# Row softmax on one core: chunks grouped in pairs of 32 rows a partition, with one paired load and one paired store

## The chip, the cores and the metric

The kernel runs on one core of one Trainium2 chip. The metric is the device time of one execution in microseconds. The engines that matter are the vector engine (DVE), the scalar engine (ACT), the sync engine (SP), which here only issues DMAs, and the 16 DMA engines that move data between the device memory (HBM) and the on-chip memory (SBUF, 128 partitions). DMAs issued from SP go through one DMA queue (q1 in the profile), those issued from ACT through another (q10).

## The reference

The input is a float32 tensor of 16 x 1024 rows of 512 numbers, 33.55 MB; the output has the same shape. Each row gets a softmax at temperature 0.5:

```python
def reference(x):
    temp = 0.5
    x_scaled = x / temp
    x_max = np.max(x_scaled, axis=-1, keepdims=True)
    exp_x = np.exp(x_scaled - x_max)
    return (exp_x / np.sum(exp_x, axis=-1, keepdims=True)).astype(np.float32)
```

## The kernel before

The 16384 rows are cut into 8 chunks of 2048 rows. In a chunk, each of the 128 partitions holds G = 16 consecutive rows of 512 numbers, so one chunk is 4 MiB, and one partition's part of it is one contiguous piece of 32 KiB in HBM. This text counts chunks from 0, as the code does; the wording "chunks 5+6" of the change's author counts from 1 and means chunks 4 and 5 here, and "chunks 3+4" means 2 and 3.

The tables at the top of the kernel say how each chunk is moved and worked on. `LOADS` cuts chunk 0 into two loads, rows 0 to 4 and 4 to 16; every other chunk is one load. `BLOCKS` cuts chunk 0 into three blocks of work and chunk 7 into two; the rest are one block each, 11 blocks in all. `STORES` has one store a chunk. Six chunk buffers exist (`BUFS = 6`), and results overwrite the input in place; chunks 6 and 7 reuse the buffers of chunks 0 and 1, so their loads wait for the stores of these chunks.

For each block, four steps follow each other:

- `shift`: issues the chunk's loads from SP when the chunk is first met (L66), takes the negated maximum of each row on DVE (L74), and multiplies it by 2 on DVE (L78) to make the bias;
- `exponentials`: on ACT, one instruction for each of the block's rows a partition (L86) computes exp(2x + bias) in place and leaves the sum;
- `scale_vector` and `scale_scalar`: DVE takes the reciprocal of the sums (L101) and multiplies seven eighths of the rows (L103); ACT multiplies the rest (L112);
- `store`: ACT issues the chunk's store (L120) once its last block is done.

The order is written out by hand (`manual_schedule`), and each engine works through its instructions in program order. The maxima run two blocks ahead of the scaling, and the exponentials one block ahead:

```python
    for i in range(n):
        if i + 1 < n:
            exponentials(i + 1, rows(i + 1)[0])
        scale_vector(i)
        scale_scalar(i)
        if i + 2 < n:
            shift(i + 2)
        store(i)
```

Loads are issued as early as their buffers allow: SP has nothing else to do, so the loads of chunks 0 to 5 all go out in the first microseconds and stand in line in SP's queue.

Of the kernel before, what the change touches and what calls it, by code (L numbers as in the profile page):

```python
# [1 line left out]

# [4 lines left out]


@with_exitstack
def kernel(  # L10
    ctx: ExitStack,
    tc: tile.TileContext,
    x: bass.AP,
    out: bass.AP,
):
    nc = tc.nc
    fp32 = mybir.dt.float32
    P = nc.NUM_PARTITIONS
    AX = mybir.AxisListType.X
    EXP = mybir.ActivationFunctionType.Exp  # L20
    COPY = mybir.ActivationFunctionType.Copy
    MAX = mybir.AluOpType.max

    D = x.shape[-1]
    xf = x.flatten_outer_dims()
    of = out.flatten_outer_dims()
    N = xf.shape[0]

    G = 16
    C = N // (P * G)
    assert C * P * G == N
    xr = xf.rearrange("(c p g) d -> c p g d", p=P, g=G)
    outr = of.rearrange("(c p g) d -> c p g d", p=P, g=G)
    WHOLE = [(0, G)]
    LOADS = [[(0, 4), (4, G)]] + [WHOLE] * 7
    BLOCKS = [[(0, 4), (4, 8), (8, G)]] + [WHOLE] * 6 + [[(0, 8), (8, G)]]
    STORES = [WHOLE] * 8  # L40
    BMAX = 16
    BUFS = 6

    data = ctx.enter_context(tc.tile_pool(name="data", bufs=BUFS))
    stats = ctx.enter_context(tc.tile_pool(name="stats", bufs=6))

    ctx.enter_context(tc.manual_schedule())


    warm = stats.tile([P, 1], fp32, name="warm", bufs=1)  # L50
    nc.vector.memset(warm, 0.0)  # L51
    nc.scalar.activation(out=warm, in_=warm, func=EXP)  # L52

    chunks = {}
    blocks = [(c, lo, hi) for c in range(C) for lo, hi in BLOCKS[c]]
    n = len(blocks)
    biases, sums, recips = {}, {}, {}

    def load(c):
        if c < BUFS:  # L60
            chunks[c] = data.tile([P, G, D], fp32, name="xt")
        else:
            chunks[c] = chunks[c - BUFS]
        xt = chunks[c]
        for lo, hi in LOADS[c]:
            nc.sync.dma_start(out=xt[:, lo:hi, :], in_=xr[c][:, lo:hi, :])  # L66

    def shift(i):
        c, lo, hi = blocks[i]
        if c not in chunks:  # L70
            load(c)
        b = hi - lo
        negmax = stats.tile([P, BMAX], fp32, name="negmax")
        nc.vector.tensor_reduce(  # L74
            negmax[:, 0:b], chunks[c][:, lo:hi, :], axis=AX, op=MAX, negate=True
        )
        biases[i] = stats.tile([P, BMAX], fp32, name="bias")
        nc.vector.tensor_scalar_mul(biases[i][:, 0:b], negmax[:, 0:b], 2.0)  # L78

    def exponentials(i, rows):  # L80
        c, lo, hi = blocks[i]
        if i not in sums:
            sums[i] = stats.tile([P, BMAX], fp32, name="sums")
        for g in rows:
            row = chunks[c][:, lo + g, :]
            nc.scalar.activation(  # L86
                out=row,
                in_=row,
                func=EXP,
                bias=biases[i][:, g : g + 1],  # L90
                scale=2.0,
                accum_out=sums[i][:, g : g + 1],
            )


    def scale_vector(i):
        c, lo, hi = blocks[i]
        b = hi - lo
        k = b - b // 8
        recips[i] = stats.tile([P, BMAX], fp32, name="recip")  # L100
        nc.vector.reciprocal(recips[i][:, 0:b], sums[i][:, 0:b])  # L101
        rows = chunks[c][:, lo : lo + k, :]
        nc.vector.tensor_mul(  # L103
            rows, rows, recips[i][:, 0:k].unsqueeze(2).broadcast_to((P, k, D))
        )

    def scale_scalar(i):
        c, lo, hi = blocks[i]
        b = hi - lo
        for g in range(b - b // 8, b):  # L110
            row = chunks[c][:, lo + g, :]
            nc.scalar.activation(  # L112
                out=row, in_=row, func=COPY, scale=recips[i][:, g : g + 1]
            )

    def store(i):
        c, _, end = blocks[i]
        for lo, hi in STORES[c]:
            if hi == end:
                nc.scalar.dma_start(  # L120
                    out=outr[c][:, lo:hi, :], in_=chunks[c][:, lo:hi, :]
                )

    shift(0)
    shift(1)

    def rows(i):
        c, lo, hi = blocks[i]
        cut = hi - lo - (2 if c == 1 else 0)
        return range(cut), range(cut, hi - lo)  # L130

    exponentials(0, rows(0)[0])
# [9 lines that stand above are left out]
            exponentials(i + 1, rows(i + 1)[1])  # L142


# [1 line left out]
_INS = ['x']  # L146
_OUTS = [((16, 1024, 512), 'float32')]


# [23 lines left out]
```

## Time and profile before

| quantity | value |
|---|---|
| median of 4 runs | 162.27 us (162.16 to 162.35) |
| the profiled execution's own time | 162.16 us |
| its span in the profile | 160.4 us |
| DVE busy | 134.6 us (84%) |
| ACT busy | 102.2 us (64%) |
| bytes read from HBM, written to HBM | 33.55 MB, 33.55 MB |
| mean rate over the span | 419 GB/s |
| a reduce of 16 rows a partition (L74) | 8.68 us |
| a DVE scaling of 14 rows a partition (L103) | 7.62 us |
| an exponential of one row a partition (L86) | 0.71 us, and 0.19 us for its sum |

Times inside the profile are microseconds from the start of the span. The profiled execution took 1.76 us more than its span. The profile also names, for each DMA queue, the packets, the bytes and the share of the 16 DMA engines' time that its packets took, and the trace keeps start, duration and size of every packet. "Landing" is the moment at which a DMA has reported its completion.

### The profile page before, as it was taken

The page shows a single profiled execution, that of the slowest core. Times are in us where ns is not written, and L with a number is a line of the kernel's source. Part 1 is how long each engine was busy: PE and PEld are TensorE (multiplying, and loading weights), DVE is VectorE, ACT ScalarE, POOL GpSimd, SP SyncE. Part 2 cuts the span into 40 slices and gives each one's busy share as a digit, 9 for nine tenths or more (in the row PEclk, how much of TensorE's full clock was granted, in tenths as well). Part 3 has the DMA queues.
Part 4 walks back from the last instruction along what each step waited for, and adds up shares of the span by engine and source line. Part 5 has one row for each costly group of instructions (what it writes and reads, how often), then busy time and mean ns, then how long its engine had stood idle before and what let it go on. Part 6 is the DMA issues. An engine that isn't in the chain of part 4 may idle for free.

```text
span 160.4 us, 402 instructions
## 1 busy us (share of the span) xinstructions
DVE 134.6 (84%) x45; ACT 102.2 (64%) x273; POOL 0.2 (0%) x4
## 2 busy tenths in 40 slices
DVE  0608999999999999999999999999999999957000
ACT  3072549069989963998199909991899891790000
POOL 0000000000000000000000000000000000000000
DMA  5999999999999999999999999999999999999993
GB/s 192 462 409 507 392 400 507 400 392 509 409 384 400 392 466 441 400 449 458 400 449 458 400 392 517 392 392 515 400 392 499 417 392 449 466 392 449 466 392 139
DMA packets 2450, 67.13 MB, mean 419 GB/s; under 512 B 272, under 2 KB 272, under 8 KB 272
## 3 DMA queue, kind: packets, MB, share of 16 engines
q1 hardware_dynamic: 1296, 33.56, 49.2%
q10 hardware_dynamic: 1152, 33.55, 48.5%
q14 instruction: 2, 0.02, 0.0%
HBM read 33.55 MB, written 33.55 MB: 418 GB/s over the span
## 4 chain that ended last, share of the span: by engine, by line
DVE 80%; DMA 7%; ACT 4%; issue 0%; SPq 0%
DVE negmax L74 42%; DVE xt L103 36%; DMA xt<-in_x_dram 7%; ACT xt L86 4%; DVE bias L78 1%; DVE recip L101 1%; SPq L66 0%
## 5 line engine op out<-in xcount | busy, mean ns | idle before, releaser
L86 ACT ACTIVATE xt<-xt,bias 128x512 f32<-128x512 f32 x128 | 90.4, 707 | 41.4 <-DVE bias L78 40.5
L74 DVE TENSOR_REDUCE negmax<-xt 128x16 f32<-128x8192 f32 (+2 forms) x11 | 69.9, 6352 | 9.4 <-DMA xt<-in_x_dram 9.4
L103 DVE TENSOR_TENSOR xt<-xt,recip 128x7168 f32<-128x7168 f32 (+2 forms) x11 | 62.0, 5637 | 0.4
L86 ACT ACTIVATION_READ_ACCUMULATOR xt<-xt,bias 128x1 f32 x128 | 23.8, 186 | 0.0
L112 ACT ACTIVATE xt<-xt,recip 128x512 f32<-128x512 f32 x15 | 9.9, 705 | 0.0
L101 DVE RECIPROCAL recip<-sums 128x16 f32<-128x16 f32 (+2 forms) x11 | 2.4, 218 | 1.8 <-ACT xt L86 1.8
L78 DVE TENSOR_SCALAR bias<-negmax 128x16 f32<-128x16 f32 (+2 forms) x11 | 1.9, 173 | 0.4
L52 ACT ACT_TABLE_LOAD x1 | 1.3, 1283 | 0.7 <-PEq L157 0.7
L51 DVE MEMSET warm<- 128x1 f32 x1 | 0.1, 59 | 0.8 <-PEq L157 0.8
L52 ACT ACTIVATE warm<-warm 128x1 f32<-128x1 f32 x1 | 0.2, 203 | 0.0
L157 POOL MEMSET const-bfloat16-1.0<- 128x1 bf16 x1 | 0.1, 101 | 0.0
L157 POOL MEMSET const-uint8-127<- 128x1 uint8 x1 | 0.1, 101 | 0.0
L157 POOL MEMSET const-float32-0.0<- 128x1 f32 x1 | 0.1, 98 | 0.2 <-issue 0.2
L157 POOL MEMSET const-float32-1.0<- 128x1 f32 x1 | 0.1, 98 | 0.0
## 6 DMA issues: line engine op xcount, KB each, us to landing
out_dram<-xt ACTq DMA_DIRECT2D x8, 4096.0 KB, 22.8
xt<-in_x_dram SPq DMA_DIRECT2D x7, 4096.0 KB, 30.0
xt<-in_x_dram SPq DMA_DIRECT2D x1, 3072.0 KB, 11.5
xt<-in_x_dram SPq DMA_DIRECT2D x1, 1024.0 KB, 4.7
```

The lines of the kernel that those rows point to most:

```text
L51: nc.vector.memset(warm, 0.0)
L52: nc.scalar.activation(out=warm, in_=warm, func=EXP)
L74: nc.vector.tensor_reduce(negmax[:, 0:b], chunks[c][:, lo:hi, :], axis=AX, op=MAX, negate=True)
L78: nc.vector.tensor_scalar_mul(biases[i][:, 0:b], negmax[:, 0:b], 2.0)
L86: nc.scalar.activation(out=row, in_=row, func=EXP, bias=biases[i][:, g : g + 1], scale=2.0, accum_out=sums[i][:, g : g + 1],)
L101: nc.vector.reciprocal(recips[i][:, 0:b], sums[i][:, 0:b])
L103: nc.vector.tensor_mul(rows, rows, recips[i][:, 0:k].unsqueeze(2).broadcast_to((P, k, D)))
L112: nc.scalar.activation(out=row, in_=row, func=COPY, scale=recips[i][:, g : g + 1])
L157: nc = _bacc.Bacc("TRN2", target_bir_lowering=False, num_devices=1)
```

## The change

The rows are now grouped in 4 pairs of chunks. In a pair, each partition holds H = 32 consecutive rows, one contiguous piece of 64 KiB in HBM; chunk 2k is the first half of each piece, chunk 2k + 1 the second half. So a chunk that is moved by itself is now 128 pieces of 32 KiB whose starts lie 64 KiB apart in HBM. The buffers become 3 of pair size, the same memory as 6 of chunk size.

Two transfers are made as whole pairs: chunks 4 and 5 are loaded by one DMA (`PAIR` in `LOADS`), and chunks 2 and 3 are stored by one DMA (`PAIR` in `STORES`), issued when chunk 3 is done. All other transfers stay as they were in size and number. The reductions, exponentials and scalings keep their shapes and their order on every engine; only which rows of the tensor a chunk holds has changed. On ACT's list of instructions the store after chunk 2 is gone and the one after chunk 3 is of pair size; on SP's list, one load of pair size stands where two of chunk size stood.

```diff
+    H = 2 * G
-    xr = xf.rearrange("(c p g) d -> c p g d", p=P, g=G)
-    outr = of.rearrange("(c p g) d -> c p g d", p=P, g=G)
+    xr = xf.rearrange("(c p g) d -> c p g d", p=P, g=H)
+    outr = of.rearrange("(c p g) d -> c p g d", p=P, g=H)
     WHOLE = [(0, G)]
-    LOADS = [[(0, 4), (4, G)]] + [WHOLE] * 7
+    CHUNKS = [(0, G), (G, H)]
+    PAIR = [(0, H)]
+    LOADS = [[(0, 4), (4, G), (G, H)], CHUNKS, PAIR, CHUNKS]
...
-    STORES = [WHOLE] * 8
+    STORES = [CHUNKS, PAIR, CHUNKS, CHUNKS]
     BMAX = 16
-    BUFS = 6
+    BUFS = 3
...
     def load(c):
-        if c < BUFS:
-            chunks[c] = data.tile([P, G, D], fp32, name="xt")
-        else:
-            chunks[c] = chunks[c - BUFS]
-        xt = chunks[c]
-        for lo, hi in LOADS[c]:
-            nc.sync.dma_start(out=xt[:, lo:hi, :], in_=xr[c][:, lo:hi, :])
+        pair, at = c // 2, c % 2 * G
+        if pair not in pairs:
+            if pair < BUFS:
+                pairs[pair] = data.tile([P, H, D], fp32, name="xt")
+            else:
+                pairs[pair] = pairs[pair - BUFS]
+        xt = pairs[pair]
+        for lo, hi in LOADS[pair]:
+            if lo < at + G and hi > at and (pair, lo) not in loaded:
+                loaded.add((pair, lo))
+                nc.sync.dma_start(out=xt[:, lo:hi, :], in_=xr[pair][:, lo:hi, :])
+        chunks[c] = xt[:, at : at + G, :]
...
     def store(i):
         c, _, end = blocks[i]
-        for lo, hi in STORES[c]:
-            if hi == end:
+        pair, at = c // 2, c % 2 * G
+        for lo, hi in STORES[pair]:
+            if hi == at + end:
                 nc.scalar.dma_start(
-                    out=outr[c][:, lo:hi, :], in_=chunks[c][:, lo:hi, :]
+                    out=outr[pair][:, lo:hi, :], in_=pairs[pair][:, lo:hi, :]
                 )
```

More of the change, by code (lines that the diff above doesn't have):

```diff
@@ L52 @@
     nc.scalar.activation(out=warm, in_=warm, func=EXP)
-    chunks = {}
+    pairs, chunks, loaded = {}, {}, set()
     blocks = [(c, lo, hi) for c in range(C) for lo, hi in BLOCKS[c]]
```

## The prediction

> Chunks are counted from 0 as in the code. **Pair load** is the 8 MiB load of chunks 4 and 5, **pair store** the 8 MiB store of chunks 2 and 3; "store 0" is the store of chunk 0.
>
> **What bounds the kernel now.** First the page: busy time by engine, the slices, the queues.
>
> ```profile
> span 160.4 us, 402 instructions
> DVE 134.6 (84%) x45; ACT 102.2 (64%) x273; POOL 0.2 (0%) x4
> DMA  5999999999999999999999999999999999999993
> q1 hardware_dynamic: 1296, 33.56, 49.2%
> q10 hardware_dynamic: 1152, 33.55, 48.5%
> ```
>
> DVE has 16% to spare, the 16 DMA engines almost nothing: loads (q1) and stores (q10) fill 49.2% + 48.5% = 97.7% of 16 engines over the span, 156.7 us of 160.4. The other 3.7 us are the lead-in (the first packet runs at 1.7 us), the 1.2 us after the last packet (159.2), and scraps. Bytes alone set a time: 67.1 MB at the 435 GB/s of the undisturbed stages below is 154.3 us. So only a change in the rate, or idle DMA time, can move the end.
>
> The counts give the unit. q1 has 9 DMAs of 128 rows, and 16 small packets for each: 9x128 + 9x16 = 1296; q10 is 8x128 + 8x16 = 1152. One contiguous row, 8, 24 or 32 KiB, is one packet. In the trace's packet records a 32 KiB packet takes 1.213 us, an engine runs one at a time, and each DMA gives each engine 8 of them. While both queues have work an engine takes a load row, a store row, a load row in turn.
>
> Next the windows by stage (us, DVE and ACT busy, clock, DMA share, GB/s):
>
> ```profile
> 2.00:44.00 42.00, 33.54 (x15) 22.40 (x63) 0.00 (x0) 1.00 1.01 435
> 44.00:48.00 4.00, 3.93 (x4) 3.31 (x9) 0.00 (x0) 1.00 1.09 393
> 48.00:52.00 4.00, 4.00 (x1) 4.00 (x13) 0.00 (x0) 1.00 0.91 393
> 52.00:70.00 18.00, 17.93 (x5) 14.00 (x39) 0.00 (x0) 1.00 1.01 437
> 92.00:116.00 24.00, 23.86 (x8) 15.99 (x44) 0.00 (x0) 1.00 1.01 437
> ```
>
> One dent: as store 0 starts (issued at 44.0), 393 instead of 435 GB/s for 8 us, 8 x 42/435 = 0.77 us lost; there 27 load packets took 1.3 to 1.9 us.
>
> Last the DVE timeline about the pair load, the loads' landing times and the last issue:
>
> ```profile
> 62.99 7.62 DVE L103 TENSOR_TENSOR xt<-xt,recip 128x7168 f32<-128x7168 f32 x1
> 70.53 8.68 DVE L74 TENSOR_REDUCE negmax<-xt 128x16 f32<-128x8192 f32 x1
> 87.15 8.68 DVE L74 TENSOR_REDUCE negmax<-xt 128x16 f32<-128x8192 f32 x1
> ...
> DMA to landing us min/median/max: 4.7/28.8/72.9
> ...
> 147.37 0.34 ACTq L120 DMA_DIRECT2D out_dram<-xt  x1
> ```
>
> The reduce at 70.53 is chunk 4's, that at 87.15 chunk 5's. Chunk 4 landed at 57.3 (trace), chunk 5 at 76.7 (issued at 3.7, the 72.9 of the line). From 12.7 to 141 DVE never waits for data, so a delay of d at 70.53 would move the last store's issue, 147.37, by d. That store's packets start from 148.3 to 149.5, each engine as it finishes store 6. Hence the last engine allows some 1.2 us of d before idle DMA time appears.
>
> **The change part by part.**
>
> *Compute.* Instructions, shapes and order on DVE and ACT stay; ACT loses one store issue (0.34 us) at 75.5, where it then waits 4.0 us for the next bias. Zero. On SP the six loads of chunks 0 to 5 still go out by 4 us; the pair load waits for nothing. Chunk 6 still waits for store 0 alone, chunk 7 for store 1: the pair store holds a buffer nobody reuses, so its lateness delays no load.
>
> *Fewer, larger packets.* 2 x 128 packets vanish, 16 an engine. The common times are 0.309 us for 8 KiB, 0.912 for 24 and 1.213 for 32: 0.0377 per KiB both times, and 0.008 us a packet besides. So 64 KiB should take 2.42, and 16 x 0.008 = 0.1 us of each engine's time is saved. Where the saved time has no fixed part after all, it is 0; I take 0.1.
>
> *Two DMAs less.* Stores 4 to 7 run alone at the end, and their first packets are 9.68 us apart, which is 8 x 1.21: back to back, no gap. Zero. The Trainium skill ("DMA: Bandwidth & Descriptors", Anatomy of one DMA) gives each DMA about 2.0 us of fixed cost; two fewer would make 158.3, but the spacing shows this cost hidden wherever another DMA is queued.
>
> *The pair load lands as one.* With equal shares it lands when chunk 5 did, 76.7, too late for 70.53. But if one row is still one packet and turns go by packet, the load now gets 64 KiB for each 32 KiB of store. An engine, from 41.3: store 0's first turn came 4.2 us after issue, behind two more load rows. If those are one long row, three are done by 48.6 and five remain, 5 x (2.43 + 1.21) = 18.2, end 66.8; if two long rows, four by 51.0, end 65.6. Plus the dent 0.77 and chunk 5's 1.5 from last packet to landing: 67.9 to 69.1, up to 69.5 with 0.4 of spread between engines. Needed at 70.53: 1.0 to 2.6 us in hand. Zero.
>
> *Store 0 pays.* It ends when both are done, about 41.3 + 8x2.43 + 8x1.21 + 0.8 = 71.2, landing near 72.7 instead of 67.9; chunk 6's load goes out 5 us later, but finds the queues emptier. Store 1 and half of chunk 6 run to about 86, chunk 7's load is issued at 87.5, chunk 6 ends at 90.5 and lands at 92 (before: 96.0; needed at 103.8). Chunk 7 is queued 3 us ahead: no gap.
>
> *The pair store comes late.* Store 2 went out at 75.5; now it goes with store 3 at 92.1. Is DMA idle meanwhile? All loads and stores 0 and 1 are 41.9 MB, 96.4 us at 435, busy to about 99 even without the pair store. After 92.1 it takes two thirds of each engine from chunk 7, which has four rows left at 95: 4 x 3.64 = 14.6, landing near 111.4 (before 116.1; needed 120.4). The pair store ends near 119.6 with store 4 queued since 108.7; stores 5, 6 and 7 are issued at 125.3, 132.9 and 147.4 for turns at 129.3, 139.0 and 148.7, as before. Zero.
>
> *HBM addresses.* Every other transfer now takes its 32 KiB from rows 64 KiB apart, not 32. No row has a 64 KiB pitch. Nearest: first-load pieces of 8 KiB at a 32 KiB pitch took 0.309, a quarter of 1.213 but for the 0.008 a packet; gaps cost nothing there. From the other end, the worst slowing the trace has is the 393 of 435. If it held for the 50.3 MB outside the pair DMAs, their 115.7 us would grow by 12. I take zero. The skill (same page, Latency and other measured facts) speaks against the change here: rows 512 KiB apart copied at 207 GB/s where a padded pitch gave 214. By that 3% it would be 167; its smallest pitch is eight times this one, and no run here shows it.
>
> Sum: span 160.4 - 0.1. That execution took 162.16 (1.76 outside the span), so 162.06; the median of the runs is 0.11 above it, which makes the forecast 162.2.
>
> **The rivals.**
>
> *Shares by bytes, or rows cut into 32 KiB packets.* Then the pair load lands at 76.7, DVE waits 76.7 - 70.53 = 6.2 us, and everything after, the last store included, slides by 6.2 less up to 1.2 of slack: 167.3 to 168.5. It decides once the landing passes 71.7 (70.53 + 1.2); later by one us costs one us. Against it: a packet holds its engine for its whole duration, and rows of all three sizes stayed whole. For it: before, both queues had equal rows, so packets and bytes can't be told apart. With partial stalls, 0.15.
>
> *A queue that restarts loses a dent each time.* The 0.77 us were lost when store packets first entered a running stream of loads. Before, neither queue ran dry afterwards until loads ended. Now loads are absent from about 67 to 74 and stores from about 86 to 95, so each re-enters beside the other. One dent gives 162.2 + 0.8 = 163.0, two 163.8. Against it: the dent may belong to the first store alone, and single missed turns at DMA ends (66 us) show none. 0.24.
>
> *Faster.* The dent shrinks or vanishes when long rows stand before the first store, together with the 0.1 us above: 161.4 to 161.9. Against it: nothing in the trace says that the dent depends on row length. 0.12.
>
> *HBM pitch*, up to the bound above, mostly a few us: 0.04. That rows are split, and the change then is less than it says, sits in the first rival.
>
> **How the numbers follow.** No change keeps 0.45, being what DMA saturation and the landing sum give together; a measurement tells about 0.2% (0.32 us) from nothing. Faster 0.12; slower 0.24 + 0.15 + 0.04 = 0.43. No change and the dents run to 163.8, small stalls a little further: the range 161.6 to 165.0 leaves out full stalls (about 0.12), the large pitch costs (0.02) and the lowest of faster (0.03). The likeliest case alone is 161.95 to 162.6.
>
> **What would show it.** Packets: q1 should fall to 8 x 144 = 1152 and q10 to 7 x 144 = 1008; 128 more means split rows. Chunk 4's reduce should start at 70.5 with no wait on a load; a start near 76.7 is the first rival. GB/s below 435 at 72 to 76 or 92 to 97 is the second; a lower rate in all stages, or chunk 1 landing after 22.4, the pitch. The last store should be issued at 147.4 and land at 159.5. I am wrong if DMA shows idle time after 119 us, or if the end moves with no such dent.

## The result, and the profile after

The changed kernel takes 162.98 us (median of 33 runs, 162.16 to 163.92) against 162.31 (53 runs, 162.03 to 162.73): 0.39% slower, ratio 1.0039, 95% interval 1.003 to 1.0048. The likeliest case, no change at 162.2, did not come; the time is that of the second rival with one dent, 163.0. The spread says as much as the median: before, all runs lie within 0.7 us, after, within 1.8 us. Some executions of the changed kernel pay nothing, others up to 1.6 us. The profiled one took 163.37 us with a span of 161.6, 1.2 us longer than before.

From the page of the changed kernel, busy time and queues (packets, MB, share of 16 engines):

```profile
span 161.6 us, 398 instructions
DVE 134.6 (83%) x45; ACT 102.2 (63%) x273; POOL 0.2 (0%) x4
q1 hardware_dynamic: 1152, 33.55, 49.2%
q10 hardware_dynamic: 1008, 33.55, 48.1%
```

The engines' work is unchanged. The packet counts are the forecast ones for whole rows, 8 x 144 and 7 x 144: a 64 KiB row is one packet, and the packet records give it 2.418 us where the prediction had 2.42.

DVE's timeline about the pair load, the loads' landing times, what DVE waited for, and the last store's issue:

```profile
62.86 7.62 DVE L111 TENSOR_TENSOR xt<-xt,recip 128x7168 f32<-128x7168 f32 x1
70.40 8.68 DVE L82 TENSOR_REDUCE negmax<-xt 128x16 f32<-128x8192 f32 x1
...
DMA to landing us min/median/max: 4.5/23.7/66.5
...
DVE negmax L82 <- DMA xt<-in_x_dram: 9.2, 2, 4.8
...
147.25 0.34 ACTq L129 DMA_DIRECT2D out_dram<-xt  x1
```

Chunk 4's reduce starts at 70.40 with no wait. The pair load was issued at 3.3 and landed 66.5 us later, at 69.7: 0.7 us in hand. DVE's waits for loads are the two of the lead-in, and the last store is issued at 147.25, where it was at 147.37. So nothing was late up to the last issue; the loss is in the DMA time.

The packet records show where. For each I take the time above that packet's common one (0.309 us for 8 KiB, 0.912 for 24, 1.213 for 32, 2.418 for 64), add up what stands out, and divide it by the 16 engines. Following packets from end to start gives each engine's own line, a matching, not a record.

- At 45.7 to 46.5, as store 0 starts: 1.12 us an engine, one stretched 64 KiB row on each. Before: 0.73, in 32 KiB rows.
- At 90.6 to 95.6, as the pair store starts: 0.21 us an engine in the mean, but unevenly, in six rows of chunk 7's load. The matching puts three of them on one engine, 0.506 + 0.456 + 1.087 = 2.05 us. Before there is nothing of the kind near 92.
- The last packets of the 16 engines end from 158.18 to 160.38; before, from 157.97 to 159.18. By the matching, the engine that ends last is the one with the three stretched rows. The execution ends with its slowest engine. The mean rate doesn't show a loss on so few engines: from 88 to 100 us it is 427 GB/s here and 424 before (lines below).

### The profile page after: what moved, and what is told of

It is laid out like the page before. It is cut to its first block, busy times and chain, and to the rows that moved or that the text cites. A ratio compares the mean times of both kernels' runs of the same rounds, so it can differ in the third digit from the quotient of the medians.

```text
span 161.6 us, 398 instructions
## 1 busy us (share of the span) xinstructions
DVE 134.6 (83%) x45; ACT 102.2 (63%) x273; POOL 0.2 (0%) x4
## 3 DMA queue, kind: packets, MB, share of 16 engines
q1 hardware_dynamic: 1152, 33.55, 49.2%
## 4 chain that ended last, share of the span: by engine, by line
DVE 79%; DMA 7%; ACT 4%; issue 0%; SPq 0%
DVE negmax L82 41%; DVE xt L111 36%; DMA xt<-in_x_dram 7%; ACT xt L94 4%; DVE bias L86 1%; DVE recip L109 1%; SPq L73 0%
## 6 DMA issues: line engine op xcount, KB each, us to landing
xt<-in_x_dram SPq DMA_DIRECT2D x1, 66.5
```

## The experiments

Every experiment keeps the rows in pairs, as in the changed kernel, and edits its tables. "Dent" is such stretched load time, the mean over the 16 engines, from the one profiled execution; the times and ratios are from all runs. Left out is one row near 97 to 99 us that is stretched by about 0.25 us in each of these profiles, right after a packet of the instruction queue (last section).

| run | time, us | ratio (95%) | dent near 46 | dent at 90 to 97 |
|---|---|---|---|---|
| changed kernel | 162.98 | 1.0039 (1.003 to 1.0048) | 1.12 | 0.21, uneven |
| layout_only | 162.33 | 1.0003 (0.9994 to 1.0012) | 1.00 | none |
| pair_load_only | 162.41 | 1.0016 (1.0001 to 1.0031) | 1.05 | none |
| pair_store_only | 162.61 | 1.0029 (1.0011 to 1.0048) | 1.11 | 1.34 |
| store2_held | 162.38 | 1.001 (1.0001 to 1.0018) | 1.04 | none |
| dry_then_32k | 162.60 | 1.0018 (1.0008 to 1.0029) | 0.95 | 0.07, on one engine |
| filled_queue | 162.32 | 1.0004 (0.9996 to 1.0013) | 1.02 | none |
| changed_but_filled | 162.44 | 1.0008 (0.9999 to 1.0016) | 1.10 | none |
| pair_load_dry_32k | 162.88 | 1.004 (1.002 to 1.006) | 1.15 | 0.16, on a few engines |

**The parts of the change, one by one.** First the layout alone:

```diff
-    LOADS = [[(0, 4), (4, G), (G, H)], CHUNKS, PAIR, CHUNKS]
+    LOADS = [[(0, 4), (4, G), (G, H)], CHUNKS, CHUNKS, CHUNKS]
-    STORES = [CHUNKS, PAIR, CHUNKS, CHUNKS]
+    STORES = [CHUNKS, CHUNKS, CHUNKS, CHUNKS]
```

> Rows grouped in pairs of chunks as in the changed kernel (64 KiB pitch in HBM), but every load and store is one chunk again. Theory (two dents): the pitch costs nothing, so 162.3 (ratio to the kernel before within 0.1% of 1), one dent at 44 to 49 us of about 0.7 us an engine in packets of 32 KiB, none near 94. Rival (pitch): most of the +0.67 us of the change is here, about 162.9, with long packets in all stages.

It gave 162.33. Row starts 64 KiB apart cost no time that can be measured. Its first dent, with 32 KiB rows, was 1.00 us. Pair load and pair store alone have one of the two lines each:

> Only the load of chunks 4 and 5 is one DMA; stores are chunks. Theory (two dents): the dent at store 0's start grows from 0.73 to 1.12 us an engine because the packet in flight is 64 KiB; store 2 goes out at 75.5, so the store queue never runs dry and there is no dent near 94: 162.31 + 0.4 = 162.7. Rival (only the restart of the store queue costs): 162.3. Rival (all of it is the long load rows, the restart being harmless): 163.0.

It gave 162.41, a small cost whose interval almost touches none; one of its eleven runs took 163.77, the others 162.25 to 162.63. The expected growth of the first dent from 0.73 to 1.12 falls: five runs here with 32 KiB rows in flight had 0.95 to 1.11 there. Whether the one profile of the kernel before, with 0.73, lay at the low end or the new layout makes this dent larger is not shown.

> Only the store of chunks 2 and 3 is one DMA; loads are chunks. Theory (two dents): first dent as before, 0.73 us an engine in 32 KiB packets; the store queue is empty from about 87 to 93 and its return hits chunk 7's load unevenly, up to 1 to 2 us on one engine: 162.31 + 0.3 to 0.7 = 162.6 to 163.0. Rival (long load rows alone cost): 162.3.

It gave 162.61 with runs up to 163.96, most of the change's cost. Its profiled execution (163.52 us) shows the second dent in full. The windows from 88 to 100 us (DVE and ACT busy, clock, DMA share, GB/s) of the kernel before, of the changed kernel (with 92 to 97 besides), of this run, and of the run with the queue kept filled, told below:

```profile
88.00:100.00 12.00, 11.93 (x4) 8.00 (x22) 0.00 (x0) 1.00 0.98 424
```

```profile
88.00:100.00 12.00, 11.93 (x4) 8.00 (x21) 0.00 (x0) 1.00 1.01 427
92.00:97.00 5.00, 4.93 (x4) 1.06 (x3) 0.00 (x0) 1.00 1.17 492
```

```profile
88.00:100.00 12.00, 11.93 (x4) 7.99 (x21) 0.00 (x0) 1.00 1.01 388
```

```profile
88.00:100.00 12.00, 11.93 (x4) 7.99 (x21) 0.00 (x0) 1.00 1.02 436
```

Where the others move 424 to 436 GB/s, the pair store's arrival leaves 388 in this run, with the engines counted as busy all the same: the time is inside the packets. It is 1.34 us an engine, and up to 2.0 on one.

**Empty queue or long rows?** The pair store differs in two things: its rows are 64 KiB, and it comes after the store queue has been empty, from store 1's last packet at 86.3 to the issue at 92. The first try at holding store 2 back without a pair:

```diff
-            if hi == at + end:
+            if hi == at + end if pair != 1 else at + end == H:
```

> No pair DMA at all: the store of chunk 2 is merely issued later, right before the store of chunk 3, as two DMAs of 32 KiB rows. Theory (two dents): the restart of the store queue costs what it costs with a pair store, 162.6 to 163.0, with long load packets at 92 to 97. Rival (the 64 KiB store rows themselves cost, by uneven turns at the end of chunk 7): 162.3.

The expectation missed, since the edit did less than meant: ACT issued the held store at 87.3, ahead of the scaling that stands before it in the program (90.7 to 92.0), so the queue was empty for 1.1 us only. No second dent, 162.38. To really empty the queue, the condition was kept and chunk 3's store was put in front of chunk 2's, so that both wait for chunk 3:

```diff
+    STORES = [CHUNKS, CHUNKS[::-1], CHUNKS, CHUNKS]
```

> No pair DMA; the stores of chunks 3 and 2 are both issued at 92, two DMAs of 32 KiB rows, so that the store queue really is empty from about 86 to 92 (in the run with store 2 held it was issued at 87.3 and the queue was hardly empty). Theory A (an empty store queue that comes back beside running loads costs a dent of load time): stretched load packets from about 91 to 96, a wide spread of times as with the pair store, median 162.6 to 163.0. Theory B (it takes 64 KiB store rows): no second dent, 162.3 to 162.4.

It gave 162.60, with runs from 162.16 to 163.22: the empty queue costs with 32 KiB rows too, and with the same kind of spread. The counterpart keeps long rows and fills the queue:

```diff
+    STORES = [CHUNKS, [(0, 4), (4, H)], CHUNKS, CHUNKS]
-            if hi == at + end:
+            if hi == at + end or (at, end, hi) == (0, G, 4):
```

> The store of chunks 2 and 3 is cut in two: the first 4 rows a partition (8 KiB pieces) go out at 75.5 and keep the store queue from running empty, the other 28 rows (56 KiB pieces) go out at 92. Theory A (empty queue): no second dent, 162.3 to 162.4 with a narrow spread. Theory B (long store rows): dent at 91 to 96 and 162.6 to 163.0 as with the pair store.

It gave 162.32, runs from 162.25 to 162.65. The 1 MiB filler was issued at 70.7, not 75.5 as expected, and its 8 KiB packets took their turns between chunk 6's and 7's rows from 87 to 100. The big store was issued at 92.05 as in the changed kernel, in the same place of chunk 7's load, with rows nearly as long, and no dent followed. So neither the late issue nor the long store rows cost: the empty queue does. The same filler in the changed kernel itself, pair load and all:

> The changed kernel with one thing undone: the first 4 rows a partition of chunk 2 are stored at 75.5, so that the store queue never runs empty before loads end; the pair load and the other 28 rows of the pair store (56 KiB pieces) stay. Theory A (the empty store queue is the cause): no dent at 91 to 97, times 162.3 to 162.5 with a narrow spread, 0.5 to 0.7 us under the changed kernel. Rival (the 64 KiB load rows carry part of it): 162.6 to 162.8.

It gave 162.44. One MiB issued earlier takes the cost from 0.39% (0.30 to 0.48) to 0.08% (-0.01 to 0.16). Little is left to the pair load, though its own run allows more (up to 0.31%). The cross-check, pair load with an empty queue and 32 KiB store rows:

> Pair load, and both stores of chunks 2 and 3 held to 92 but as two DMAs of 32 KiB rows: the changed kernel without long store rows. If the length of the store rows adds nothing to the empty queue: 162.9 to 163.0, like the changed kernel. If it does: near 162.6, like the run with an empty queue and 32 KiB rows alone.

It gave 162.88, like the changed kernel, again with a wide spread (162.31 to 164.48, one far out). With an empty queue, 64 KiB store rows add nothing on top that these runs can tell. Whether the pair load makes the second dent larger (162.88 and 162.98 with it, 162.60 and 162.61 without) stays open: the intervals overlap.

**What the first dent is.** Three runs asked whether it follows the length of the rows in flight, and whether it belongs to the program's first store alone.

```diff
+    QUARTERS = [(0, 4), (4, 8), (8, 12), (12, G), (G, H)]
+    LOADS = [[(0, 4), (4, G), (G, H)], CHUNKS, QUARTERS, CHUNKS]
```

> No pair DMA; chunk 4, the load in flight when the first store comes, is loaded as four DMAs of 8 KiB pieces. Theory 1 (the first dent stretches the packets that are in flight, so that it grows with their length: 0.7 to 1.0 us an engine with 32 KiB, 1.1 with 64 KiB): the dent falls to 0.3 to 0.5, less 24 x 0.008 = 0.2 us an engine of packet overheads: 161.8 to 162.2. Theory 2 (the dent is a fixed time from the store's issue to its first packet): 0.7 to 1.0 us spread over many 8 KiB packets, 162.4 to 162.6.

It gave 163.40, ratio 1.0066 (1.0054 to 1.0078), outside both expectations. The dent did not shrink: some 100 packets of 8 KiB lost 1.53 us an engine. Theory 1 falls. Most of the time went elsewhere, as the DVE timeline of this run shows:

```profile
112.68 7.62 DVE L112 TENSOR_TENSOR xt<-xt,recip 128x7168 f32<-128x7168 f32 x1
122.62 4.42 DVE L83 TENSOR_REDUCE negmax<-xt 128x8 f32<-128x4096 f32 x1 [2.32 <-DMA xt<-in_x_dram]
```

Chunk 7 came 2.3 us late, and the last store was issued at 149.6 instead of 147.4. While an 8 KiB load row takes turns with a 32 KiB store row, loads get about a fifth of the engine, and every later load slid. This is the stall that the first rival feared, brought about from the other side, and it shows that shares go by packets.

```diff
+    STORES = [[(0, 4), (4, G), (G, H)], CHUNKS, CHUNKS, CHUNKS]
```

> No pair DMA; the first 4 rows of chunk 0 (8 KiB pieces) are stored as soon as they are done, at about 18, the other 12 at 44 (24 KiB pieces). Theory A (each return of an empty store queue costs): two dents, one at 19 to 22 and one at 45 to 49, 0.7 us each, 162.8 to 163.2. Rival (only the first store of the program costs): one dent, at 19 to 22, nothing at 45 to 49, 162.2 to 162.4.

It gave 162.08, ratio 0.999 (0.9981 to 1.0): the fastest median here, 0.1% under the kernel before. The windows of the kernel before, then of this run:

```profile
18.00:24.00 6.00, 5.93 (x4) 1.99 (x7) 0.00 (x0) 1.00 1.00 431
44.00:52.00 8.00, 7.93 (x4) 7.30 (x21) 0.00 (x0) 1.00 1.00 393
```

```profile
18.00:24.00 6.00, 5.93 (x4) 1.99 (x6) 0.00 (x0) 1.00 0.98 371
44.00:52.00 8.00, 7.93 (x4) 7.39 (x21) 0.00 (x0) 1.00 1.02 426
```

The dent moved with the first store, from 44 to 52 us (393) to 18 to 24 (371). At 46.7, back from being empty since 32.4, the queue cost a second one, but of 0.27 us instead of 0.7. So neither expectation holds as written: in this run the first arrival costs most and a later return less, unlike in pair_store_only (1.11 and 1.34).

```diff
+    STORES = [[(0, 4), (4, 8), (8, G), (G, H)], CHUNKS, CHUNKS, CHUNKS]
```

> No pair DMA; chunk 0 is stored in three pieces as its blocks are done (4 rows at 18, 4 at 25, 8 at 44), so that the store queue starts early and is empty for a shorter time before 44. Theory A: the dent of 0.7 us at 19 to 21 stays, the one of 0.27 at 47 to 51 shrinks, if the queue is still working at 44 it vanishes: 161.8 to 162.1, under the kernel before. Rival (two returns, two dents): 162.3 to 162.6.

Its windows:

```profile
18.00:24.00 6.00, 5.93 (x4) 1.99 (x6) 0.00 (x0) 1.00 0.98 366
44.00:52.00 8.00, 7.93 (x4) 7.45 (x21) 0.00 (x0) 1.00 1.02 438
```

The dent at 44 is gone altogether (438 GB/s; the queue was empty only from 44.9 to the first packet at 47.3, with the next store issued at 43.9), as theory A has it, yet the time was 162.35, ratio 1.0003 (0.9995 to 1.0012). DVE's timeline shows a new wait, for chunk 7's load:

```profile
121.08 4.42 DVE L82 TENSOR_REDUCE negmax<-xt 128x8 f32<-128x4096 f32 x1 [0.75 <-DMA xt<-in_x_dram]
```

With stores taking their turns from 22 us on, the loads landed later, chunk 7's at 121.05 instead of 116.07, and the last store was issued 0.7 us later, at 148.1. All but one engine ended together at 158.7 to 158.8 (from 157.97 to 158.32 in the kernel before), with no dent larger than 0.1 us after the one at 19 to 21 (0.80). The engine that ended last, at 159.32, was by the matching not held by the late issue: its last packets followed on without a gap. So the wait is one cost of storing still earlier, and why the gain of the run before it did not carry over stays open.

## Why the prediction was wrong

**What held.** DMA saturation: DVE and ACT did the same, the last issue stood still, and the time followed the DMA engines. Whole rows as packets: 1152 and 1008. The pair load: landing forecast at 67.9 to 69.5, measured 69.7, and 0.7 us in hand where 1.0 to 2.6 were forecast; had shares gone by bytes, 76.7. The turns by packet are what the Trainium skill states ("DMA: Bandwidth & Descriptors", Queues, rings and completion order); the alternation of 64 and 32 KiB rows here and the starved 8 KiB rows agree. Store 0: landing forecast near 72.7, measured 72.1; chunk 7's load issued at 87.9 (87.5); chunk 6 landed at 91.5 (92). "Two DMAs less: zero" held as far as the runs tell: pair_load_only, with one load fewer, gained nothing. The skill's 2.0 us a DMA did not show; the section that the prediction names describes DMAs issued from GpSimd, while all DMAs here are issued from SP and ACT. "HBM addresses: zero" held by layout_only. "Fewer, larger packets" is right in the packet records (2.418 us against 2 x 1.213), but its 0.1 us is too little to tell in the times.

**What failed** is the step "The pair store comes late", priced at zero. It asked only whether the DMA engines would run out of work between 86 and 92, and they did not. It charged nothing for the store queue running empty and coming back beside a running load, though the same text had the row for it, the dent of 0.77 us at the first store, and used it in the second rival alone. The runs put the price on this step: filling the empty queue takes the cost from 0.39% to 0.08%; emptying the queue without a pair DMA costs 0.18% (0.08 to 0.29). The landing of chunk 7 (forecast 111.4, measured 114.8) and the pair store's end (119.6, measured 121.7) were late on a few engines alone: by the small packets that end a DMA on each engine, eleven of the 16 had finished chunk 7 by 110.1 and the last at 114.4.

**The second rival** had the right mechanism and one wrong half. It charged each return alike, with 0.77 us on every engine. The loads' return at 75.8, beside store 1, showed no stretched packet; only the stores' return cost time here. That its sum for one dent, 163.0, meets the median is partly luck, and the sign it named, a rate below 435 GB/s at 92 to 97, did not come: that window gives 492 in the changed kernel, as it counts each packet where it starts and the loss sat on few engines. And the return is no fixed sum: 0.07 to 1.34 us an engine over four profiles, and it counts by its slowest engine, 2.05 us in the changed kernel's profile against a mean of 0.21. The weights were a mistake too: against this rival the prediction held that single missed turns at DMA ends show no dent, but in the old trace the store queue never stood empty beside loads for longer than such a turn (from 66.3 to 67.9).

**The counter-argument** that the dent might belong to the first store alone is half right: later returns are mostly smaller (0.27 in early_first_store). What inside the queue causes the dent, whether it is the return or already the empty stretch before it, and why its size differs so from run to run, these runs don't settle.

## What to carry to other kernels

Where the DMA engines are saturated, merging transfers had nothing to gain here; look for the queue that the merged transfer leaves empty meanwhile. A store held back until its queue ran dry beside a running load stream cost up to 1.3 us an engine on its return, and 1 MiB issued earlier kept that away. How long a queue must stand empty for this was not measured: about 6 us showed it, 1.1 us did not. When both queues have work, shares go by rows, so a longer contiguous row takes bandwidth from the other queue, and a shorter one gives it away.

## What was not expected of the hardware

- The stretch comes well before the first store packet: in pair_store_only the store was issued at 91.97 and its first packet ran at 96.4, but load rows that started at 90.5 to 90.9, and should have ended by 91.7 to 92.1, were already stretched by 0.15 to 0.78 us. One of them ended at 91.91, 0.16 us late and before the issue, so a part of the stretch comes ahead of the issue and is not explained by it. The first dent began at 45.9, 1.9 us after its store's issue and 2.3 us before that store's first packet (48.2), so it is not store packets entering the stream that begin it, as the prediction had read it.
- One engine ends 0.5 to 0.9 us behind the next in most profiles, that of the kernel before included (159.18 against 158.32). There, two 8 KiB packets of the instruction queue run at 37.4 and 96.9, 0.31 us each, and 0.3 us after the start of each a load row begins that is stretched by 0.36 and 0.25 us. That these 1.2 us are all on the engine that ends last fits the sum but was not tested.
- Rows are stretched at the very start too: in the profile before, 20 of the first 8 KiB load rows, from 1.7 to 2.8 us, lost 0.40 us an engine in sum, with no store in flight.
